# An encoder trunk on one core: a planner that reckons with later landing of copies between buffers and with shorter transposes, and two low parts of each layer's first quad on VectorE

## The chip, the cores and the metric

The kernel runs on 1 core of one Trainium2 chip. Five engines each run their own stream of instructions in order: TensorE (PE, with its weight loads listed as PEld), VectorE (DVE), ScalarE (ACT), GpSimd (POOL) and SyncE (SP); here POOL and SP mainly issue DMA transfers. The engines wait for each other by semaphores. The metric is the device time of one execution in microseconds; the median of several runs counts. Profiles come from one execution each.

## The reference

Two layers (DEPTH = 2) over one sequence of S = 512 tokens with D = 1024 channels, all in float32. In each layer:

```
h = rms_norm(x, attn_norm_g);  z = h @ w_in          # 1024 -> 512+128+128+512+512+512+1024+1024
qa, ka, va, qb, kb, vb, ga, gb = split(z)
qa, ka = rope(rms_norm(qa)), rope(rms_norm(ka));  qb, kb = rms_norm(qb), rms_norm(kb)
ya = window_gqa(qa, ka, va, sink) @ w_proj_a         # 8 heads of 64, 2 k/v heads, window 128
yb = neighbourhood_attn(qb, kb, vb, rel_bias) @ w_proj_b   # 8 heads, 8 x 64 grid, 8 x 16 window
x = x + (sigmoid(ga) * ya + sigmoid(gb) * yb) @ w_out
h = rms_norm(x, ffn_norm_g)
x = x + (silu(h @ w_gate) * (h @ w_up)) @ w_down     # hidden width 2816
```

## The kernel before, in words

**Precision and tiling.** Each float32 operand of a large product is split into a high part, rounded to a shorter format (fp32r), and a low part, the remainder. A product is then three matmuls on PE: high x high, high x low, low x high. x is kept transposed, 128 channels on the partitions and 512 tokens in a row. A projection goes by pairs of 128 output columns (`pair_matmul`) or by blocks of 128 tokens (`token_matmul`); weights come as slabs by DMA from POOL's queue, and their low parts by a second DMA that adds the weights onto the negated high part.

**Attention.** Head by head: scores on PE, maximum on DVE, exponential on ACT, scaling, transposes of the probabilities on PE, their split into high and low parts on ACT and DVE, products with v on PE. Two heads of 64 channels lie above each other on 128 partitions. `q_parts` puts q's high part on one half of the partitions and its low part on the other. `k_parts` (for the second branch four times a layer, for the first branch once) transposes k on PE, splits it on ACT and DVE, and then copies each of the four halves to the other half of the partitions by DMA on SP's queue:

```
Q.dma_start(kh[other].bitcast(F32), kh[own].bitcast(F32))
Q.dma_start(kl[other].bitcast(F32), kl[own].bitcast(F32))
```

Scores of the pair's first head read the first two of these copies. On SP's queue the small loads of the bias tables stand ahead of them.

**Feed-forward.** The first 256 hidden columns go as ordinary pairs (`evac_g`, `evac_u`), then five groups of 512 columns as "quads": seven products of quarter matrices in place of eight, in the order m = 1, 5, 6, 2, 7, 3, 4, for w_gate and for w_up. `Quad.high(m)` forms the sum of quarters that m needs (a11, a12, a21, a22 are the quarters of the raw weights) and rounds it on ACT; `high(6)` overwrites a21 and a11, `high(3)` overwrites a12. `Quad.low(m)` forms the low part. In most quads that is one subtraction on DVE; in the first quad's w_gate of each layer (`by_transfer`) it is `low_by_transfer`: ACT writes the negated high part, and a DMA from POOL's queue adds the source onto it, buffer to buffer. `chain_x` forms the seven sums and splits of x. On PE m = 1 and m = 5 come first; then `seed`, a COPY on ACT of the bank of m = 1, fills the bank into which m = 6 accumulates.

**What sets the order.** Nothing runs ahead of a recorded order. The function `trunk` is run twice. The first, dry run keeps a clock per engine, adds the `cost` of each operation, and notes in `ready` when each buffer is there; a DMA counts as landed some time after its bytes have moved. Beside the main stream of projection matmuls stand chains (generators: `chain_q`, `chain_kv`, `chain_pair_a`, `chain_pair_b`, `head`, `chain_x`, `chain_parts` and others). A chain yields a `Need`: the buffers, banks and events its next step wants. After each unit of three matmuls the planner issues those steps whose needs its clocks call met. So PE's order is an interleaving of projection matmuls with scores, transposes and products of the heads, chosen by the planner's costs. Weight loads, `high` and `low` hang on positions in the main stream (`at_pos`, `due`), not on clocks. The dry run also notes from when to when each buffer is used (`touch`); `Layout.pack` and `spread` then place all buffers in two arenas, in such a way that a buffer's place is not taken again at once. The second run emits the instructions in the order found.

All instructions are issued through one helper, so every row of the profile names its line, L308. Names tell rows apart: `arena` is either arena, `mm` are PSUM banks of projections, `at` PSUM banks of the attention and of transposes and m = 1 and 5, `cst` the constants with the identity.

Of the kernel before, what the change touches and what calls it, by code (L numbers as in the profile page):

```python
# [213 lines left out]
def trunk(ctx: ExitStack, tc: tile.TileContext, a: dict, out: bass.AP, lay: Layout):  # L214
# [20 lines left out]
    def buf(shape, dtype=F32):  # L235

        n = int(np.prod(shape))
        x = lay.place(n, dtype)
        t = arenas[dtype][:, x : x + n]
        if len(shape) == 2:  # L240
            t = t.rearrange("p (a b) -> p a b", b=shape[1])
        elif len(shape) == 3:
            t = t.rearrange("p (a b c) -> p a b c", b=shape[1], c=shape[2])
        return t

    def name_of(ap):
        return lay.owner(ap.offset) if ap.tensor.name in arena_names else ap.tensor.name
# [17 lines left out]
    ready = {}  # L265
    HOPS = {("pe", "dve"): 0.2, ("pe", "act"): 0.2, ("dve", "pe"): 0.26, ("act", "pe"): 0.3, ("dve", "dve"): 0.06}

    def at_(tensor, key):

        t, by = ready.get(tensor, (0.0, key))  # L270
        return t + HOPS.get((by, key), 0.0 if by == key else 0.15)


    def cost(eng, name, o, aps):
        n = max(x.free_size() for x in aps) / 1000.0
        in_psum = any(x.space == PS for x in aps[1:])
        if eng == "pe":
            cols = aps[2].free_size()
            if name == "transpose":
                return 0.11  # L280
            if aps[1].dtype == F32:
                return max(4 * cols, 256) / 2400.0 + 0.002
            return 0.12 if cols == 256 else (cols if cols >= 256 else 4 * cols) / 2255.0
        if eng == "act":
            return n * 0.833 + (0.06 if in_psum else 0.1) + 0.093 * sum(x.free_size() == 1 for x in aps[2:])
        if eng == "dve":
            fast = name in ("tensor_copy", "tensor_scalar") and not in_psum
            return n * (0.52 if fast else 6.4 if name == "reciprocal" else 1.04) + 0.075
        return n * 2.2 + 0.1
# [3 lines left out]
    def touch(aps, start, end):  # L293
        for x in aps:
            o = name_of(x)
            if isinstance(o, int):
                lay.touch(o, steps[0], start, end)

    class Engine:
# [3 lines left out]
        def __getattr__(self, name):  # L303
            f = getattr(self.eng, name)

            def call(*args, **kw):
                if not lay.dry:
                    f(*args, **kw)  # L308
                    return
                aps = [x for x in (*args, *kw.values()) if isinstance(x, bass.AP)]  # L310
                acc = kw.get("accum_out") if "accum_out" in kw else (args[7] if name == "tensor_tensor_reduce" else None)
                steps[0] += 1
                start = max([clock[self.key]] + [at_(name_of(x), self.key) for x in aps[1:]])
                if self.key == "dma":
                    start = max(start, clock["pe"] - 3.0)
                    if self.eng is nc.gpsimd:
                        clock["pool"] += 1.0
                    end = start + aps[0].free_size() * aps[0].shape[0] * 4 / 360e3
                    clock["dma"] = end
                    ready[name_of(aps[0])] = end + 2.0, "dma"  # L320
                    touch(aps, start, end + 2.0)
                    return
                end = start + cost(self.key, name, aps[0], aps)
                clock[self.key] = end
                ready[name_of(aps[0])] = end, self.key
                if acc is not None:
                    ready[name_of(acc)] = end, self.key
                touch(aps, start, end)

            return call  # L330
# [201 lines left out]
    def low_by_transfer(lo, src, h):  # L532

        A.activation(lo, h.bitcast(F32), AF.Copy, scale=-1.0)
        GQ.dma_start(lo, src, accum_op=ALU.add)

    class Quad:
# [37 lines left out]
        def low(self, m):  # L575
            src, h = self.parts[m]
            lo = buf([4, 256], F32R)
            if self.by_transfer:
                low_by_transfer(lo, src, h)
            else:  # L580
                V.tensor_tensor(lo, src, h.bitcast(F32), ALU.subtract)
            self.parts[m] = h, lo
# [503 lines left out]
    def layer(l):  # L1086
# [273 lines left out]
        def chain_x():  # L1360
# [26 lines left out]
            high(1, b11)  # L1387
            V.tensor_tensor(n1, b11, b12, ALU.subtract)
            yield from low(1)
            high(5, n1)  # L1390
            yield from normal(1)
            V.scalar_tensor_tensor(n2, n1, -1.0, b22, ALU.mult, ALU.subtract)
            high(6, n2)
            yield from low(5)
            yield from low(6)
            high(2, b21)
            yield from low(2)
# [194 lines left out]
```

## Time and profile before

| | |
|---|---|
| runs | 1484.63, 1482.7 and 1477.24 us, median 1482.7 |
| profiled execution | 1478.58 us, span 1476.8 us |
| mean granted PE clock | 0.983 |
| PE busy | 1405.2 us, 95% of the span |
| DVE, ACT, POOL busy | 62%, 48%, 25% |
| PE waits for ACT at `mm`, for copies between buffers at `at` | 24.9 us in 2 waits, 12.3 us in 7 waits |

In a row of a group or a timeline stand start and length in us (timeline), engine, operation, what it writes and reads with sizes, a count, and in brackets how long its engine was idle just before and what ended that. In a table of windows the last three columns are PE's granted clock (1.00 is full speed), the share of the DMA engines and GB/s. The span leaves out 1.8 us of the execution.

### The profile page before, as it was taken

The numbers are of one execution on the slowest core, as the hardware profiler recorded it, in microseconds if no ns is written. First come the engines' busy times: TensorE is split into PE (matmuls) and PEld (weight loads), VectorE is DVE, ScalarE is ACT, GpSimd is POOL, SyncE is SP. The second block draws the span as 40 slices with busy tenths as digits, with TensorE's granted clock in tenths as the row PEclk, the third lists the DMA queues.
The fourth block names the chain that finished last, engine by engine and source line by source line (L and its number), as shares of the span: only waits on it lengthen the run. The fifth ranks groups of instructions, "written<-read, shape, count | busy, mean of one in ns | idle before, by whom it ended". The sixth has DMA issues, their size and how long they took to land.

```text
span 1476.8 us, 21019 instructions
## 1 busy us (share of the span) xinstructions
PE 1405.2 (95%) x8074; PEld 1230.7 (83%) x8074; DVE 908.5 (62%) x1743; ACT 713.9 (48%) x1200; POOL 368.6 (25%) x374
## 2 busy tenths in 40 slices
PE   5999989999969999999999999999997999999998
PEld 4778878888869999999987887788886899999997
DVE  3876768543747565575647868673437575575653
ACT  3476657543544343433545775574345444343431
POOL 4533222234221110201353322123332211101111
PEclk9999999999989999999999999899999899999999
DMA  9877778899975745645798679669997754836455
GB/s 228 164 145 137 145 128 150 153 191 241 174 150 119 174 115 143 158 100 117 154 189 168 125 132 158 124 122 183 209 242 130 160 124 122 190 83 168 115 100 114
DMA packets 211427, 223.18 MB, mean 151 GB/s; under 512 B 25964, under 2 KB 179744, under 8 KB 211328
## 3 DMA queue, kind: packets, MB, share of 16 engines
q0 software_dynamic: 159920, 167.23, 61.1%
q1 hardware_dynamic: 51408, 54.62, 13.3%
q8 instruction: 63, 1.03, 0.3%
q14 instruction: 36, 0.29, 0.1%
HBM read 207.13 MB, written 2.10 MB: 142 GB/s over the span
## 4 chain that ended last, share of the span: by engine, by line
PE 69%; DMA 9%; DVE 9%; issue 7%; ACT 4%; POOL 2%; DVEq 0%; POOLq 0%; ACTq 0%; SPq 0%
PE mm L308 50%; PE at L308 19%; DVE arena L308 6%; ACT arena L308 4%; DMA arena<-arena 3%; DMA arena<-in_w_out 2%; DVE sm L308 2%; POOL arena L308 2%; DMA arena<-in_w_gate 1%; DMA arena<-in_w_up 1%; DMA arena<-in_rel_bias_b 1%; DMA vec<-in_q_norm_b 1%; DMA arena<-in_w_in 0%; ACT L308 0%; DVE hf L308 0%
## 5 line engine op out<-in xcount | busy, mean ns | idle before, releaser
L308 PE MATMUL mm<-arena 128*128 128x512 f32 (+1 forms) x5568 | 1127.9, 358 | 32.0 <-ACT mm L308 24.9
L308 PEld LDWEIGHTS mm<-arena 128*128 128x128 f32 x5568 | 910.1, 191 | 161.7 <-ACT mm L308 25.3
L308 PE MATMUL at<-arena 128*128 128x256 f32 (+2 forms) x1952 | 309.4, 299 | 15.1 <-DMA arena<-arena 12.3
L308 ACT ACTIVATE arena<-arena 128x1024 fp32r<-128x1024 f32 (+3 forms) x280 | 235.9, 865 | 176.9 <-DMA arena<-in_w_down 62.2
L308 ACT CAST arena<-arena 128x1024 fp32r<-128x1024 f32 (+2 forms) x250 | 211.7, 864 | 224.0 <-DVE arena L308 219.5
L308 PEld LDWEIGHTS at<-arena 128*128 128x128 f32 x1952 | 268.7, 193 | 38.7 <-DMA arena<-arena 11.9
L308 DVE TENSOR_TENSOR arena<-arena,arena 128x1024 fp32r<-128x1024 f32 (+2 forms) x236 | 228.3, 981 | 57.3 <-ACT arena L308 57.1
L308 POOL DMA_DIRECT2D arena<-in_w_in x168 | 168.4, 1367 | 368.3 <-ACT arena L308 367.9
L308 DVE TENSOR_TENSOR arena<-arena,mm 128x512 f32<-128x512 f32 x144 | 98.8, 686 | 255.9 <-PE mm L308 255.8
L308 POOL DMA_DIRECT2D arena<-in_w_down x96 | 98.2, 1210 | 503.2 <-ACT arena L308 388.4
L308 DVE TENSOR_TENSOR arena<-arena 128x1024 f32<-128x1024 f32 (+3 forms) x196 | 158.8, 824 | 19.2 <-DMA arena<-arena 14.1
L308 DVE TENSOR_TENSOR arena<-at,arena 128x384 fp32r<-128x384 f32 (+4 forms) x206 | 114.1, 562 | 52.7 <-ACT arena L308 45.9
L308 ACT CAST arena<-at 128x384 fp32r<-128x384 f32 (+2 forms) x164 | 74.4, 459 | 117.5 <-PE at L308 105.1
L308 PE MATMUL at<-cst,arena 128*128 128x128 f32 x504 | 87.4, 280 | 11.8 <-DVE arena L308 7.9
L308 PEld LDWEIGHTS at<-cst,arena 128*128 128x128 f32 x504 | 64.5, 143 | 30.5 <-DVE arena L308 10.9
L308 ACT ACTIVATE arena<-arena,negm 128x256 f32<-128x256 f32 (+1 forms) x128 | 71.6, 561 | 13.1 <-DVE negm L308 12.7
L308 DVE TENSOR_TENSOR arena<-mm,arena 128x512 f32<-128x512 f32 x72 | 49.3, 687 | 45.8 <-PE mm L308 45.7
L308 ACT COPY arena<-at 64x512 f32<-64x512 f32 (+1 forms) x60 | 34.8, 581 | 64.8 <-PE at L308 64.3
L308 POOL DMA_DIRECT2D arena<-in_w_out x32 | 35.2, 1292 | 54.5 <-ACT arena L308 54.5
L308 DVE CUSTOM_DVE_ANT_0 arena<-at,arena 128x256 f32<-128x256 f32 (+1 forms) x64 | 31.0, 486 | 28.7 <-PE at L308 28.4
L308 DVE CUSTOM_DVE_ANT_0 arena<-at,cst,nsnk 128x256 f32<-128x256 f32 (+1 forms) x64 | 34.3, 546 | 16.3 <-PE at L308 15.9
L308 DVE TENSOR_SCALAR arena<-arena,sm 128x384 f32<-128x384 f32 (+1 forms) x97 | 34.0, 405 | 1.1
(70 smaller groups left out, 444.2 us busy)
## 6 DMA issues: line engine op xcount, KB each, us to landing
arena<-in_w_in POOLq DMA_DIRECT2D x104, 512.0 KB, 7.1
arena<-in_w_down POOLq DMA_DIRECT2D x80, 512.0 KB, 6.8
arena<-in_w_gate SPq DMA_DIRECT2D x20, 1024.0 KB, 6.7
arena<-in_w_up SPq DMA_DIRECT2D x20, 1024.0 KB, 5.2
arena<-in_w_in POOLq DMA_DIRECT2D x64, 256.0 KB, 6.2
arena<-in_w_out POOLq DMA_DIRECT2D x32, 512.0 KB, 8.0
arena<-in_w_proj_a POOLq DMA_DIRECT2D x16, 512.0 KB, 8.8
arena<-in_w_proj_b POOLq DMA_DIRECT2D x16, 512.0 KB, 6.5
```

The source lines that it names most:

```text
L308: f(*args, **kw)
```

## The change

Three edits. In the planner's cost table a transpose counts 0.1 in place of 0.11 us. In its handling of a DMA, the result counts as there 7.0 us after its bytes have moved where the source is a buffer on the chip; from DRAM it stays 2.0. And in the quads with `by_transfer`, which is the first quad's w_gate in each layer, m = 1 and m = 2 get their low part by the subtraction on DVE, while 5, 6, 7, 3 and 4 stay with ACT and a DMA.

```diff
@@ -277,7 +277,7 @@
             if name == "transpose":
-                return 0.11
+                return 0.1
@@ -317,8 +317,9 @@
                     clock["dma"] = end
-                    ready[name_of(aps[0])] = end + 2.0, "dma"
-                    touch(aps, start, end + 2.0)
+                    end += 2.0 if aps[1].space == bass.MemoryType.DRAM else 7.0
+                    ready[name_of(aps[0])] = end, "dma"
+                    touch(aps, start, end)
                     return
@@ -575,7 +576,7 @@
             lo = buf([4, 256], F32R)
-            if self.by_transfer:
+            if self.by_transfer and m not in (1, 2):
                 low_by_transfer(lo, src, h)
             else:
                 V.tensor_tensor(lo, src, h.bitcast(F32), ALU.subtract)
```

The first two edits change no instruction, only the order and the places of buffers. In the attention this is PE's order before at the second branch's second pair in layer 0. `at ... <-cst` are transposes (the first row is k's tile), `mm` projection matmuls, `at` of 128x256 to 128x512 scores and products of heads, and the last row is the first score that reads this k:

```order
L308 MATMUL at_1857<-cst,arena_72 128x128 x4
L308 MATMUL mm_1837<-arena_73 128x512 x3
L308 MATMUL at_1869<-arena_73 128x512 x2
L308 MATMUL at_1872<-cst,arena_72 128x128 x2
L308 MATMUL mm_1837<-arena_73 128x512 x3
L308 MATMUL mm_1838<-arena_73 128x512 x6
L308 MATMUL at_1869<-arena_73 128x256 x2
L308 MATMUL at_1893<-cst,arena_72 128x128 x3
L308 MATMUL mm_1838<-arena_73 128x512 x6
L308 MATMUL at_1915<-arena_73 128x256 x2
```

And after, the same pair, from k's transposes on:

```order
L308 MATMUL at_1790<-cst,arena_72 128x128 x4
L308 MATMUL at_1795<-arena_73 128x512 x2
L308 MATMUL at_1798<-cst,arena_72 128x128 x2
L308 MATMUL mm_1662<-arena_73 128x512 x3
L308 MATMUL at_1809<-arena_73 128x384 x2
L308 MATMUL mm_1662<-arena_73 128x512 x3
L308 MATMUL at_1795<-arena_73 128x256 x2
```

then 14 rows of the same kinds, and these up to the first scores of that k:

```order
L308 MATMUL mm_1839<-arena_73 128x512 x6
L308 MATMUL mm_1838<-arena_73 128x512 x3
L308 MATMUL at_1889<-arena_73 128x256 x2
L308 MATMUL at_1912<-cst,arena_72 128x128 x3
L308 MATMUL at_1917<-arena_73 128x256 x2
```

Between the first and the last row there were 18 projection matmuls, and now there are 36; with them stand 16 products and scores (4 of 512 columns, 4 of 384, 8 of 256) in place of 4 (2 of 512, 2 of 256), and 15 transposes in place of 5. The k tile's transposes come earlier in the stream, the scores at much the same place. At the end of layer 0's attention the last head's last product stood 48 projection matmuls ahead of w_proj_a's first, and now 21.

At the first quad of layer 0, DVE before, from the evacuation of w_gate's ordinary pair on. The two rows of 128x1024 that write arena_73 are low parts of x, the first 128x4x256 is the add of `high(3)`, the rows with `mm` after it evacuate w_up's ordinary pair:

```order
L308 TENSOR_TENSOR arena_72<-mm_3281,arena_72 128x512
L308 TENSOR_TENSOR arena_72<-mm_3282,arena_72 128x512
L308 TENSOR_TENSOR arena_73<-arena_72,arena_73 128x1024 x2
L308 TENSOR_TENSOR arena_72<-arena_72 128x4x256
L308 TENSOR_TENSOR arena_72<-mm_3392,arena_72 128x512
L308 TENSOR_TENSOR arena_72<-arena_72 128x512
L308 TENSOR_TENSOR arena_73<-arena_72,arena_73 128x512
L308 TENSOR_TENSOR arena_73<-arena_72,arena_73 128x1024
L308 TENSOR_TENSOR arena_72<-arena_72 128x4x256
L308 TENSOR_TENSOR arena_72<-mm_3393,arena_72 128x512
```

And after:

```order
L308 TENSOR_TENSOR arena_72<-mm_3280,arena_72 128x512
L308 TENSOR_TENSOR arena_72<-mm_3281,arena_72 128x512
L308 TENSOR_TENSOR arena_73<-arena_72,arena_73 128x1024 x4
L308 TENSOR_TENSOR arena_72<-arena_72 128x4x256 x2
L308 TENSOR_TENSOR arena_72<-mm_3391,arena_72 128x512
L308 TENSOR_TENSOR arena_72<-arena_72 128x512
L308 TENSOR_TENSOR arena_73<-arena_72,arena_73 128x512
L308 TENSOR_TENSOR arena_72<-mm_3392,arena_72 128x512
```

`low(2)` stands at the head of a row of four low parts, and one low part of x and one subtraction of `chain_x` have moved ahead of w_up's evacuations. ACT at the same place before, up to the COPY that seeds the bank of m = 6; the first ACTIVATE row is the two Silu, the ACTIVATE rows of 128x1024 are negated high parts:

```order
L308 ACT_TABLE_LOAD
L308 ACTIVATE arena_72<-arena_72 128x512 x2
L308 ACTIVATE arena_73<-arena_73 128x1024
L308 CAST arena_73<-arena_72 128x1024 x2
L308 ACTIVATE arena_73<-arena_73 128x1024
L308 CAST arena_73<-arena_72 128x1024
L308 CAST arena_73<-arena_72 128x512
L308 ACTIVATE arena_73<-arena_73 128x1024
L308 CAST arena_73<-arena_72 128x1024
L308 CAST arena_73<-arena_72 128x512
L308 CAST arena_73<-arena_72 128x1024 x2
L308 COPY mm_3500<-at_3466 128x512
```

And after:

```order
L308 ACT_TABLE_LOAD
L308 ACTIVATE arena_72<-arena_72 128x512 x2
L308 CAST arena_73<-arena_72 128x1024 x2
L308 ACTIVATE arena_73<-arena_73 128x1024
L308 CAST arena_73<-arena_72 128x1024 x2
L308 CAST arena_73<-arena_72 128x512
L308 ACTIVATE arena_73<-arena_73 128x1024
L308 CAST arena_73<-arena_72 128x512
L308 CAST arena_73<-arena_72 128x1024
L308 COPY mm_3496<-at_3464 128x512
```

Two instructions fewer stand ahead of the COPY: the activation of `low(2)` and one cast of 128x1024, which now follows the COPY. On POOL's queue the copies from buffer to buffer around the quad go from seven to five. Layer 1 has the same order at this place.

## The prediction

> **What bounds the kernel now.** I read the page first, then the table of waits, then single stretches of the timeline with the granted clock beside them. The page's head, its busy times and the shares of the chain that ended last:
>
> ```profile
> span 1476.8 us, 21019 instructions
> PE 1405.2 (95%) x8074; PEld 1230.7 (83%) x8074; DVE 908.5 (62%) x1743; ACT 713.9 (48%) x1200; POOL 368.6 (25%) x374
> PE 69%; DMA 9%; DVE 9%; issue 7%; ACT 4%; POOL 2%; DVEq 0%; POOLq 0%; ACTq 0%; SPq 0%
> ```
>
> PE is busy for 1405.2 of 1476.8 us. The change takes no matmul away and adds none, so it can only win from the 71.6 us in which PE stands, and from stretches in which PE runs at a lower clock after it stood. The waits of PE that the change can touch (us in total, times, longest):
>
> ```profile
> PE mm L308 <- ACT mm L308: 24.9, 2, 12.5
> PE at L308 <- DVE arena L308: 12.5, 20, 2.1
> PE at L308 <- DMA arena<-arena: 12.3, 7, 4.2
> ```
>
> Two places carry 37.2 us of PE's idle time: two waits of 12.5 us, one in each layer's first quad, and seven waits for copies between buffers, all in the attention. The first stands like this in layer 0 (timeline; start, length, engine):
>
> ```profile
> 403.04 1.28 DVE L308 TENSOR_TENSOR arena<-mm,arena 128x512 f32<-128x512 f32 x2
> 404.23 1.28 ACT L308 ACT_TABLE_LOAD   x1
> 404.23 2.35 DVE L308 TENSOR_TENSOR arena<-arena,arena 128x1024 fp32r<-128x1024 f32 x2
> 405.52 2.10 ACT L308 ACTIVATE arena<-arena 128x512 f32<-128x512 f32 x3
> 406.06 5.91 PE L308 MATMUL at<-arena 128*128 128x256 f32 x48
> 407.53 1.98 ACT L308 CAST arena<-arena 128x1024 fp32r<-128x1024 f32 x2
> 408.00 1.28 POOL L308 DMA_DIRECT2D arena<-arena  x1 [10.78 <-ACT arena L308]
> 409.41 1.05 ACT L308 ACTIVATE arena<-arena 128x1024 fp32r<-128x1024 f32 x1
> 413.53 1.22 DVE L308 TENSOR_TENSOR arena<-arena 128x1024 f32<-128x1024 f32 x1 [6.94 <-DMA arena<-arena]
> 414.67 0.68 DVE L308 TENSOR_TENSOR arena<-mm,arena 128x512 f32<-128x512 f32 x1
> 415.46 0.69 DVE L308 TENSOR_TENSOR arena<-arena 128x512 f32<-128x512 f32 x1
> 416.19 0.62 ACT L308 CAST arena<-arena 128x512 fp32r<-128x512 f32 x1 [0.31 <-DVE arena L308]
> 423.74 0.57 ACT L308 COPY mm<-at 128x512 f32<-128x512 f32 x1
> 424.36 5.49 PE L308 MATMUL mm<-arena 128*128 128x256 f32 x24 [12.39 <-ACT mm L308]
> ```
>
> DVE stops for 6.94 us until 413.53. What stands there is the add of `high(3)`, which overwrites a12; the copy issued at 408.00 still reads a12 for `low(2)`. Behind the add on DVE wait the two evacuations of w_up's first pair, behind them casts on ACT, and behind those the COPY that seeds the bank of m=6. PE finishes m=1 and m=5 at 411.97 (406.06 + 5.91) and stands until 424.36.
>
> The second place, at a k pair of layer 0 and at two of layer 1 (timeline), and what the chain of waits shows ahead of the first and the last of them:
>
> ```profile
> 195.88 0.60 PE L308 MATMUL at<-cst,arena 128*128 128x128 f32 x4
> 202.66 0.35 PE L308 MATMUL at<-arena 128*128 128x256 f32 x1 [0.77 <-DMA arena<-arena]
> 207.18 0.58 PE L308 MATMUL at<-arena 128*128 128x256 f32 x1 [4.17 <-DMA arena<-arena]
> ```
> ```profile
> 917.69 0.35 PE L308 MATMUL at<-arena 128*128 128x256 f32 x1 [1.42 <-DMA arena<-arena]
> 919.73 0.58 PE L308 MATMUL at<-arena 128*128 128x256 f32 x1 [1.68 <-DMA arena<-arena]
> 950.14 0.58 PE L308 MATMUL at<-arena 128*128 128x256 f32 x1 [3.20 <-DMA arena<-arena]
> ```
> ```profile
> 199.30 7.84 DMA arena<-arena
> ...
> 943.54 7.43 DMA arena<-arena
> ```
>
> k is transposed at 195.88, and the last copied half has landed at 207.14 (199.30 + 7.84): 11.3 us, of which 7.84 is the copy. The next scores need it and PE stands. These three pairs hold nearly all of the 12.3 us. After such a stop PE's granted clock (last but two in a row) is halved for a while:
>
> ```profile
> 207.00:209.00 2.00, 1.82 (x5) 1.53 (x6) 0.43 (x2) 0.00 (x0) 0.00 (x0) 0.50 0.38 57
> 211.00:212.00 1.00, 1.00 (x4) 0.81 (x3) 0.45 (x2) 1.00 (x3) 0.00 (x0) 0.53 0.32 51
> 424.00:430.00 6.00, 5.64 (x26) 5.64 (x27) 2.15 (x3) 3.33 (x5) 3.20 (x3) 0.50 0.52 119
> 921.00:925.00 4.00, 4.00 (x14) 3.64 (x13) 1.89 (x6) 1.81 (x6) 0.00 (x0) 0.50 1.10 219
> 925.00:927.00 2.00, 2.00 (x12) 1.76 (x11) 0.43 (x2) 0.72 (x3) 0.00 (x0) 0.92 0.02 4
> 953.00:956.00 3.00, 3.00 (x11) 2.52 (x11) 0.79 (x3) 1.38 (x4) 0.00 (x0) 0.50 1.11 238
> ```
>
> **The attention.** The new landing of 7.0 us and the transposes' 0.1 us change no instruction of it, only the order. Counted in the order shown with the change, PE had 18 matmuls of 512 columns, 2 score matmuls of 512 and 2 of 256, and 5 transposes between this k's transposes and its first scores; now it has 36, 2+2 of 512, 4 of 384, 8 of 256 and 15 transposes. Their durations:
>
> ```profile
> 284.68 18.54 PE L308 MATMUL mm<-arena 128*128 128x512 f32 x81
> 444.28 2.92 PE L308 MATMUL at<-arena 128*128 128x256 f32 x23
> ```
>
> That is 0.229 us for 512 columns and 0.127 for 256; 384 lie between, at 0.18, and a transpose of 128 columns is put at 0.09 (below 0.127). Before: 20 x 0.229 + 2 x 0.127 + 5 x 0.09 = 5.3 us. Now: 40 x 0.229 + 4 x 0.18 + 8 x 0.127 + 15 x 0.09 = 12.2 us. Needed were 11.3 at this pair, the longest copy that I found on the chain. The other late pairs go from 5.3 to 6.5 and 7.8 us up to 10.6 and 12.9 by the same count. So six of seven waits go. The half clock behind them goes too: 4.7 us at this pair (207.18 to about 211.9), 5.6 at the second (919.73 to about 925.3), and about as much at the third (950.14 to 956 at the least). Half of 15.9 us is lost, 8.0. Term: 12.3 + 8.0 = 20.3, less about 1.3 for the pair with 10.6 us of cover, 19.0. Bounds: 0 if the copies land later by as much as they are given, 20.3 if all goes; below nothing it goes only by new waits, a rival below.
>
> What is late next is the end of the attention: the last head's products now end 21 matmuls of 0.229 us (4.8 us) ahead of the first product of w_proj_a, where it were 48 in layer 0. The last head's parts are read only 24 matmuls later, by w_proj_b, so 45 x 0.229 = 10.3 us cover the last copy, add, cast and subtraction (four steps of 0.6 to 0.7 us, by the 512-column rows above, with 0.2 between). That stays hidden, at 0. On SP's queue the copies stay behind the same bias loads as before. The dry run also places all buffers of both arenas anew; a buffer that then comes free too late would be a new wait, and as nothing here shows one, I put it at 0 (the lost cover would be one of the rivals' stops, below).
>
> The skill has a rule on this clock. The Trainium skill, TensorE: Matmul & The Clock Gate, section "What's actually happening", says that an idle window of about 3.4 us halves the clock and about 3.4 us of work bring it back. The 4.7 to 5.6 us of these rows are longer; by that page each of the three stops would give back 1.7 us in place of 2.7, and the sum would be 27.6 and the time 1455.1.
>
> **The first quad.** Per layer it removes two ACT activations of 1.05 us, two POOL issues of 1.28 and two copies of 512 KB from buffer to buffer, and adds two DVE subtractions of 1.2. The removed ones lie beside PE's matmuls, on engines that are busy 48% and 25%: 0. `low(1)` falls where DVE waits for PE anyway:
>
> ```profile
> 382.60 0.69 DVE L308 TENSOR_TENSOR arena<-arena,mm 128x512 f32<-128x512 f32 x1 [2.03 <-PE mm L308]
> ```
>
> 2.03 us cover 1.2, so 0; without that cover 1.2 on a DVE that has idle time before 403. `low(2)` lands on the path, in front of x's lows. With the rows above, on DVE: evacuations end 404.3; three lows of 1.18 end 407.8; the fourth waits for the two casts of ACT, which lost the activation ahead of them (405.52, two Silu of the three rows' 2.10 less 1.05, and 1.98: 408.6) and ends 409.8; two adds of 1.17 end 412.1, the first of which waits for no copy any more; evacuation and product 0.68 + 0.69, 413.5; cast 0.62, 414.2; subtraction 0.7, 414.9; the second evacuation and product, 416.3; cast 417.0; a CAST of 1.04, 418.0; COPY 0.57, 418.6. PE goes on at 418.6 in place of 424.36: 5.8 us per layer, 11.6 in all (the wait of layer 1 is 12.5). 6.6 us of waiting stay, and I let the half clock after it stay as it is. Bounds per layer: -2.4 (both subtractions on the path, and the add held by something else) to 12.4 plus half of the 6 us at half clock, 15.4. I take 5.8, since each of its steps has a row.
>
> **Sum.** 19.0 + 11.6 = 30.6 us. The profiled execution's own time is 1478.6, 1.8 above its span, and stands 4.1 under the median of 1482.7. Against the execution it gives 1448; against the median, 1452.1. I forecast 1452.
>
> **Rivals.**
> - Only the quad gains. For it: the median copy of 128 KB is quick (last number), and where one is late something else may delay it.
>
> ```profile
> arena<-arena POOLq DMA_DIRECT2D x14, 512.0 KB, 6.9
> arena<-arena SPq DMA_DIRECT2D x40, 128.0 KB, 3.2
> ```
>
> Then cover of 5.3 us would have done, the late copies are late by what shares the rings and queues with them, and the new order runs into that again. 1482.7 - 11.6 = 1471. [...] Against: the chain ends in copies of 7.43 and 7.84 at the late pairs, and it is these that count. 0.15.
> - Only the attention gains: the add finds another thing to wait for (the cast of a11 or the raw weights), and 12.4 stays. 1482.7 - 19 = 1464. Against: DVE's wait in the row names the copy. 0.09.
> - The change does nothing: each wait passes to the next thing. 1482. 0.05.
> - Slower: the new order puts more heads' steps at once on DVE, and PE waits there for scores and products in the middle of the attention. PE already waits 20 times for DVE, by 0.6 us on average. A longer stop costs what these did, (12.3 + 8.0) / 3 = 6.8 us with its clock; five of them eat 34, and from six on (41) it is slower by over half a per cent: 1452 + 41 = 1493. Against: the number of DVE and ACT instructions in the attention is the same, and DVE is busy 62%. 0.10.
> - Better: in the quad nearly all goes, the clock too, 9 us more per layer: 1434. 0.04.
>
> **How the numbers follow.** The forecast itself has 0.57, with its own range from 1446 to 1460: 20 or 16 in the attention, 2 us either way per quad, and the 4 us between execution and median. For 8 in 10 the range goes from 1444 to 1474 and takes in the two half gains, 0.57 + 0.15 + 0.09. Half a per cent, 7.4 us, is about what a measurement of this kernel can tell from no change. Faster: 0.57 + 0.15 + 0.09 + 0.04 = 0.85; same 0.05; slower 0.10.
>
> **What would show it.** Right: among PE's waits the copies are down from 12.3 to under 2 us, and the clock after k's first scores is whole; DVE has no wait for a copy at the first quad; PE's wait for the seeding COPY is 6 to 7 us in both layers, still with half clock behind. Wrong: PE's waits for DVE or ACT in the attention grow by more than 10 us, or the copies take as much longer as they are issued earlier; or in the quad another engine's row stands ahead of the COPY. If PE's busy time grows although the matmuls are the same, the clock fell somewhere new.

## The result, and the profile after

The changed kernel takes 1444.7 us (median of four runs, 1439.9 to 1445.1) against 1482.1 before (four runs, one more than above, 1477.2 to 1484.6): a ratio of 0.974, 95% interval 0.9716 to 0.9764, or 37.4 us less by the medians. 1452 was forecast, 31 us less; the medians lie at the low end of the range, and 0.974 times 1482.1 is 1443.6, just under it. Two executions of kernels tested below, of 1969 and 3562 us, took far longer than all others of their kernels and are in no median. The two profiled executions are 1478.6 and 1444.7 us long, their spans 33.9 us apart. The page's head of the kernel after, its busy times and the shares of its chain:

```profile
span 1442.9 us, 20988 instructions
PE 1394.6 (97%) x8074; PEld 1224.6 (85%) x8074; DVE 912.2 (63%) x1752; ACT 706.8 (49%) x1191; POOL 363.4 (25%) x370
PE 77%; DVE 12%; issue 3%; DMA 3%; ACT 3%; POOL 1%; DVEq 0%; POOLq 0%; ACTq 0%
```

PE stands for 48.3 us (1442.9 less 1394.6) where it stood for 71.6, and it is busy 10.6 us less with the same matmuls, most of it because fewer of them ran at half clock (8.3 us, below). Its waits (us in total, times, longest):

```profile
PE mm L308 <- ACT mm L308: 12.5, 2, 6.3
PE at L308 <- DVE arena L308: 11.5, 15, 2.3
```

The row of PE waiting for copies between buffers, 12.3 us before, is gone, and the two waits for the seeding COPY are half as long. At the attention's pair that stood for 4.17 us before, PE now works through at full clock (table of windows, granted clock last but two):

```profile
203.00:207.00 4.00, 4.00 (x22) 3.54 (x21) 3.05 (x12) 3.54 (x10) 2.03 (x2) 1.00 0.59 122
207.00:209.00 2.00, 2.00 (x13) 1.67 (x12) 1.97 (x8) 1.47 (x4) 0.00 (x0) 1.00 1.03 145
```

The first quad of layer 0 (timeline):

```profile
396.30 1.28 DVE L308 TENSOR_TENSOR arena<-mm,arena 128x512 f32<-128x512 f32 x2
...
397.50 3.48 DVE L308 TENSOR_TENSOR arena<-arena,arena 128x1024 fp32r<-128x1024 f32 x3
...
399.53 5.91 PE L308 MATMUL at<-arena 128*128 128x256 f32 x48
399.84 1.98 ACT L308 CAST arena<-arena 128x1024 fp32r<-128x1024 f32 x2
...
401.85 1.22 DVE L308 TENSOR_TENSOR arena<-arena,arena 128x1024 fp32r<-128x1024 f32 x1 [0.87 <-ACT arena L308]
402.99 2.35 DVE L308 TENSOR_TENSOR arena<-arena 128x1024 f32<-128x1024 f32 x2
...
405.26 0.68 DVE L308 TENSOR_TENSOR arena<-mm,arena 128x512 f32<-128x512 f32 x1
...
410.99 0.57 ACT L308 COPY mm<-at 128x512 f32<-128x512 f32 x1
...
411.61 5.49 PE L308 MATMUL mm<-arena 128*128 128x256 f32 x24 [6.17 <-ACT mm L308]
```

DVE goes from the evacuations through four low parts and two adds to w_up's evacuation without a wait for a copy. Between the two profiles the waits fell by 24.7 us (12.3 for copies, 12.4 for the COPY). The time that PE's work lost to half clock, added up over windows of 2 us as busy time times one less the granted clock, fell from 14.0 to 5.7 us, by 8.3. That is 33.0 of the 33.9 us. Behind the two waits for the COPY the half clock stayed (6.0 us of PE's work lost there before, 5.7 now). One stop is longer than before: ahead of the second norm's sums of squares in layer 0, PE stands 2.34 us at 380.33, where it stood 0.26.

### The profile page after: what moved, and what is told of

The parts are those of the page before. It is cut to its first block, busy times and chain, and to the rows that moved or that the text cites. A ratio compares the mean times of both kernels' runs of the same rounds, so it can differ in the third digit from the quotient of the medians.

```text
span 1442.9 us, 20988 instructions
## 1 busy us (share of the span) xinstructions
PE 1394.6 (97%) x8074; PEld 1224.6 (85%) x8074; DVE 912.2 (63%) x1752; ACT 706.8 (49%) x1191; POOL 363.4 (25%) x370
## 4 chain that ended last, share of the span: by engine, by line
PE 77%; DVE 12%; issue 3%; DMA 3%; ACT 3%; POOL 1%; DVEq 0%; POOLq 0%; ACTq 0%
PE mm L308 60%; PE at L308 18%; DVE arena L308 9%; ACT arena L308 3%; DVE sm L308 3%; DMA arena<-in_w_in 2%; DMA arena<-in_w_up 1%; POOL arena L308 1%; DMA cst<-in_consts 1%; DVE hf L308 0%; DVE den L308 0%; ACT L308 0%; ACT mm L308 0%; ACT sm L308 0%; DVEq L308 0%
## 5 line engine op out<-in xcount | busy, mean ns | idle before, releaser
L308 PE MATMUL mm<-arena 128*128 128x512 f32 (+1 forms) x5568 | 1123.6, 357 | 20.7 <-ACT mm L308 12.5
L308 ACT ACTIVATE arena<-arena 128x1024 fp32r<-128x1024 f32 (+3 forms) x276 | 232.7, 862 | 188.8 <-DMA arena<-in_w_down 58.9
L308 PE MATMUL at<-arena 128*128 128x256 f32 (+2 forms) x1952 | 303.8, 296 | 5.0 <-DVE arena L308 3.5
L308 PEld LDWEIGHTS at<-arena 128*128 128x128 f32 x1952 | 265.7, 191 | 25.9 <-DVE arena L308 8.1
L308 DVE TENSOR_TENSOR arena<-arena,arena 128x1024 fp32r<-128x1024 f32 (+2 forms) x240 | 233.0, 984 | 59.7 <-ACT arena L308 59.3
L308 DVE TENSOR_SCALAR arena<-arena,sm 128x384 f32<-128x384 f32 (+1 forms) x102 | 33.9, 387 | 1.1
```

## The experiments

**Each edit alone.** The three edits are put into the kernel before one by one.

```diff
-            if self.by_transfer:
+            if self.by_transfer and m not in (1, 2):
```

> Kernel before with the quad edit alone: low(1) and low(2) of the first w_gate quad on DVE, the planner's numbers as before. My theory (two separate gains that add up): PE's two waits for the seeding COPY fall from 12.4 to 6.2 us each and nothing else moves, since the edit saves no clock there; the attention keeps its waits for copies. That is 12.4 us, a ratio of about 0.992. Rival (the quad gains only where the order of the attention was repaired too, or the run after gains by the new places of the buffers): the waits for the COPY stay above 10 us and the time is within 0.3% of before.

1467.0 us against 1482.3 in the same session, a ratio of 0.9902 (0.9871 to 0.9933). The gain, 15.3 us by the medians, is what was expected or somewhat more. A second profile of this kernel:

> The kernel with the quad edit alone, profiled a second time, since the granted clock of its first profile was 0.658 throughout. The edit gained 14.5 us by the timed runs where I gave it 12.4. My theory: the waits for the COPY are about 6.2 us each and the waits for k copies 11 to 15 us as in the kernel before. Rival: the waits for k copies have fallen too, by the new places of the buffers.

This execution was a long one, 1474.4 us. Waits of PE:

```profile
PE at L308 <- DMA arena<-arena: 15.3, 6, 4.7
PE mm L308 <- ACT mm L308: 10.1, 2, 5.0
```

The waits for the COPY fell, those for k copies did not. So the quad edit gains by itself.

```diff
-                    ready[name_of(aps[0])] = end + 2.0, "dma"
-                    touch(aps, start, end + 2.0)
+                    end += 2.0 if aps[1].space == bass.MemoryType.DRAM else 7.0
+                    ready[name_of(aps[0])] = end, "dma"
+                    touch(aps, start, end)
```

> Kernel before with the landing of 7.0 us for copies between buffers alone; transposes at 0.11, all low parts of the first quad by transfer. My theory: the seven waits of PE for copies go (12.3 us) and the half clock after them (8.3 us of PE's busy time), while the two waits of 12.4 us at the first quads stay: 20.6 us, a ratio of about 0.986. Rival (the two numbers of the planner are only right together): with the old transpose cost another order comes out, with copies that are still late or with waits for DVE, and less than 12 us are gained.

1461.7 us, 0.9867 (0.9838 to 0.9896): 20.6 us less, as expected. In its profile PE waits for no copy between buffers, and 24.4 us for the COPY. That the size is met so exactly is partly luck: between the profiles it is 17.8 us, of which 12.3 are the waits, while the half clock fell by 5.5 us (14.0 to 8.5) and not by 8.3, since some followed stops at the two norms of layer 0 in this execution.

```diff
-                return 0.11
+                return 0.1
```

> Kernel before with the transpose at 0.1 us in the planner alone. My theory: it only shifts the order a little, the k copies are planned as late as before, and all waits stay in size: within 0.4% of before, either way. Rival (this number carries the gain in the attention): the waits for copies fall by more than half and the ratio is 0.993 or less.

1473.1 us, 0.9941 (0.9923 to 0.996). My theory falls: this number gains 9 us by itself. The rival is not right either, since in the profile the waits for copies are still 10.9 us. The profiled execution took 1479.6 us, 6.5 above the median of the runs, so the kernel was profiled a second time:

> The kernel with the transpose edit alone, profiled a second time, since its first profile (1479.6 us) stood 6.5 us above the median of its runs. My theory (the first profile caught late copies of the first quads' low parts: the waits for the COPY were 15.9 us each): now they are about 12.4 us each, and the span is about 7 us shorter. Rival (the difference lies in the attention or in the clock): the COPY waits are again near 15.9 us, and the rest differs.

1469.6 us. Its waits:

```profile
PE mm L308 <- ACT mm L308: 30.2, 2, 15.2
DVE arena L308 <- DMA arena<-arena: 19.5, 4, 6.9
PE at L308 <- DMA arena<-arena: 8.6, 6, 2.8
```

The waits for the COPY are as long as in the first profile, so the difference between the two executions does not lie there, against what I expected. Against the kernel before, the copies cost 3.7 us less, PE's waits for DVE 4.8 less (7.7 for 12.5) and the half clock 6.5 less (7.5 for 14.0), and the COPY costs 5.3 more; together that is 9.7 us, and the two executions lie 9.0 apart. PE's two waits for the COPY grew by 2.8 and 2.5 us; ahead of each layer's first quad DVE now waits for one more copy between buffers (timeline), and the chain that ends in the COPY stands behind that:

```profile
395.94 2.74 DVE L308 SCALAR_TENSOR_TENSOR arena<-arena,vecT 128x512 f32<-128x512 f32 x4 [2.88 <-DMA arena<-arena]
...
1114.64 2.74 DVE L308 SCALAR_TENSOR_TENSOR arena<-arena,vecT 128x512 f32<-128x512 f32 x4 [2.78 <-DMA arena<-arena]
```

Of the waits for DVE, a stop at the start is gone. PE there sums the squares of x for the first norm (matmuls that read `ones`), first in this kernel, then in the kernel before:

```profile
42.84 1.02 PE L308 MATMUL at<-ones,arena 128*128 128x1 f32 x8
```
```profile
45.38 1.02 PE L308 MATMUL at<-ones,arena 128*128 128x1 f32 x8 [2.06 <-DVE arena L308]
```

**The kernel before, once more.**

> The kernel before, unchanged, profiled a second time. My theory (what differs between its runs is when copies between buffers land): the same PE waits at the same places, those for k copies and the two for the COPY, with sizes that differ by some us in all from the first profile's 12.3 and 24.9. Rival (the runs differ in the granted clock or at the start): these sums agree within 1 us, and the difference lies in PE's busy time or ahead of the first matmuls.

This execution is 8.2 us longer than the first profiled one (span 1485.0). The copies cost 14.5 in place of 12.3 us, the COPY 23.4 in place of 24.9, and the stop ahead of the second norm's sums in layer 0 1.91 in place of 0.26: together 2.4 us. The larger part is PE's busy time, 1410.5 in place of 1405.2. Windows behind the stop of 2.06 us at the first norm, in this execution and, at about the same place with the same stop, in the first one:

```profile
46.00:48.00 2.00, 2.00 (x10) 1.90 (x10) 1.15 (x7) 1.08 (x2) 0.61 (x1) 0.50 0.00 0
48.00:50.00 2.00, 2.00 (x6) 1.61 (x5) 1.26 (x8) 0.00 (x0) 2.00 (x4) 0.50 0.24 32
50.00:52.00 2.00, 2.00 (x6) 1.52 (x5) 1.80 (x11) 0.98 (x2) 1.35 (x2) 0.50 1.08 156
52.00:54.00 2.00, 2.00 (x10) 1.63 (x10) 0.38 (x2) 1.18 (x3) 0.00 (x0) 0.81 1.28 280
```
```profile
46.00:48.00 2.00, 2.00 (x12) 1.72 (x12) 1.21 (x8) 0.75 (x2) 1.03 (x2) 1.00 0.02 4
48.00:50.00 2.00, 2.00 (x10) 1.35 (x9) 1.69 (x12) 1.72 (x4) 2.00 (x4) 1.00 0.48 53
```

The same stop of 2.06 us brought 6.8 us at half clock in one execution (three windows of 2 us at 0.50, one at 0.81: 3.4 us lost) and none in the other. So the rival holds for the larger part, though the sums do not agree within 1 us as it asked: these two executions differ by where the half clock falls, and less by when copies land.

**Two edits together.** First the changed kernel without the landing, then without the transpose's new cost.

```diff
-                    end += 2.0 if aps[1].space == bass.MemoryType.DRAM else 7.0
+                    end += 2.0
```

> Changed kernel with the landing of copies between buffers back at 2.0 us; the transpose at 0.1 and the quad edit stay. My theory (the landing alone repairs the attention; the transpose edit gains by the start of each layer): the waits for k copies stay at 10 to 13 us, the waits for the COPY are about 12 us in two, and the ratio is 0.980 to 0.986. Rival (with the quad edit the transpose edit gains as much as both numbers): below 0.978.

1453.3 us, 0.9816 (0.9784 to 0.9849), in the range of my theory. PE waits 9.9 us in 7 times for k copies and 12.5 us for the COPY. The landing then adds 8.6 us to reach the changed kernel, where alone it gained 20.6. Against the kernel before of its own session this kernel gains 27.8 us; the quad edit alone gained 15.3, so the transposes' number brings 12.5 us here, more than alone. That fits the row above: DVE's wait of 2.9 us for a copy ahead of the quad is absent here.

```diff
-                return 0.1
+                return 0.11
```

> Changed kernel with the transpose back at 0.11 us in the planner; landing 7.0 and the quad edit stay. It completes the eight combinations of the three edits but one. Alone the transpose edit gained 9 us, and the landing gained 9 us on top of the other two but 20 alone. Theory A (both repair the same waits for k copies, so with the landing in place the transposes have little left): within 0.3% of the changed kernel. Theory B (the transposes' gain is another one, the stop of PE ahead of each norm's sums and the half clock after it, which the landing does not touch): 4 to 9 us more than the changed kernel, with stops of 1 to 2 us at the matmuls that read the ones.

1446.7 us, 0.9775 (0.975 to 0.98), against 0.974 (0.9716 to 0.9764) with it: 2 us by the medians, 5 by the ratios, 3.2 by the gains of 34.2 and 37.4 us over the kernel before of each one's own session, and the intervals overlap. How large the transpose's share is in the whole is not settled. Its stop is there again in the profile of this kernel (timeline, and the windows from 45 to 51 us):

```profile
46.27 1.73 PE L308 MATMUL at<-ones,arena 128*128 128x1 f32 x8 [2.06 <-DVE arena L308]
```
```profile
45.00:51.00 6.00, 4.73 (x16) 4.09 (x17) 4.65 (x23) 1.45 (x3) 3.15 (x4) 0.62 0.30 56
```

The stop is the one that Theory B names, and this execution, 1450.8 us, was the longest of the four. But the changed kernel has a stop of its own at the second norm's sums, 2.34 us at 380.33, where this one has 0.15, so part of the gain is given back there. In all PE stands 48.4 us here and 48.3 in the changed kernel; the two spans differ by PE's busy time.

**How much landing it takes, and low(1).**

```diff
-                    end += 2.0 if aps[1].space == bass.MemoryType.DRAM else 7.0
+                    end += 2.0 if aps[1].space == bass.MemoryType.DRAM else 4.5
```

> Changed kernel with a landing of 4.5 us in place of 7.0. My theory (each late k pair needs about 11 us between its transposes and its scores, and the landing buys that time nearly one to one): the cover falls to about 9 us and waits for copies of 2 to 6 us come back, 3 to 9 us more than the changed kernel with the half clock. Rival (any landing above the median copy of 3.2 to 4.0 us is enough): no wait for copies above 1 us in all, and the time of the changed kernel within 0.2%.

1445.3 us, 0.9777 (0.9744 to 0.9809), by the median the time of the changed kernel. PE's wait for copies:

```profile
PE at L308 <- DMA arena<-arena: 0.8, 3, 0.4
```

The rival is right. By the order and the prediction's durations, the cover at the three pairs that were late is 8.1, 7.8 and 9.3 us here, less than the 11.3 that I took to be needed, and it suffices but for 0.8 us.

```diff
-            if self.by_transfer and m not in (1, 2):
+            if self.by_transfer and m != 2:
```

> Changed kernel, but low(1) of the first w_gate quad goes by ACT and a copy again; low(2) stays on DVE. My prediction's view (low(1) lies beside PE's matmuls either way): the time is that of the changed kernel within 0.2%. Rival (the copy of low(1), which reads a11, holds the add of high(6) on DVE and with it all that DVE does ahead of the first quad; the profile with the transpose edit alone shows such a wait of 1.68 us, the kernel before one of 0.19): 2 to 5 us more than the changed kernel, with a wait of DVE for a copy between buffers ahead of the quad.

1442.6 us, 0.9757 (0.9723 to 0.9792): no difference from the changed kernel that these runs show. As far as they show, `low(1)` costs nothing either way, as predicted, and the gain of the quad edit is that of `low(2)`.

**What is left of the first quad's wait.** From here on the changed kernel is the base. First the split of w_up's ordinary pair goes later, and `chain_x` waits for the COPY to be issued:

```diff
-            h, lo = act(F32R), act(F32R)
-            split(gt[j], h, lo)
-            u.append((h, lo))
+            soon(lambda: u_parts(j), 6.0)
...
             yield from low(2)
+            yield Need(keys=[f"{key}seed"], backlog=XLOG)
```

> Changed kernel, and at the first quad the splits of w_up's ordinary pair (two casts and two subtractions of 512 columns) come 6.0 us later in the main stream, and chain_x goes on behind x's low part 2 only once the seeding COPY is issued. So on ACT two casts that wait for DVE and one of 1024 columns no longer stand ahead of the COPY. My theory (the COPY waits in ACT's queue behind work that nobody needs yet): PE's wait there falls from 6.2 to about 2.4 us, and as that is short, the half clock behind it (3 us lost per layer) goes or shrinks: 7 to 14 us less than the changed kernel, 1431 to 1438 us. Rival (the wait only moves): PE then stands as long at m=7 for x's low part 7, or at m=2, and the time is that of the changed kernel within 0.3%.

1445.7 us, 0.9771 (0.9736 to 0.9807): the wait moved. In layer 0 (timeline):

```profile
404.69 4.58 PE L308 MATMUL mm<-arena 128*128 128x256 f32 x24 [2.64 <-ACT mm L308]
...
414.75 13.13 PE L308 MATMUL mm<-arena 128*128 128x256 f32 x84 [2.57 <-DVE mm L308]
```

The wait for the COPY fell from 6.2 to 2.6 us as my theory had it, but m=7 then waits 2.6 us for the second seed, which DVE forms behind a subtraction (`seed_c`: the sum of m=6's bank and a copy of m=5's goes into the bank of m=3, and m=7 goes on in m=6's bank, so it must wait until that has been read). Half clock followed each, and nothing was won. In the next kernel three more things are put later, and `low(4)` goes on DVE:

```diff
-                early = max(0.0, early - 1.2)
+                early = max(0.0, early - 2.7)
...
-            if self.by_transfer and m not in (1, 2):
+            if self.by_transfer and m not in (1, 2, 4):
...
-            soon(lambda: u_parts(j), 6.0)
+            soon(lambda: u_parts(j), 11.0)
...
             yield from low(7)
+            yield Need(keys=[f"{key}seed_c"], backlog=XLOG)
```

> The kernel with the COPY ahead of the late splits, and three edits more: the splits come 11.0 us later in place of 6.0, chain_x's parts 3 and 4 wait until the second seed (of m=3's bank) is issued, and the first w_gate quad prepares its later parts later (the lead shrinks by 2.7 us from part to part, not by 1.2; low(4) then goes on DVE). So fewer casts stand ahead of the COPY on ACT, and fewer subtractions ahead of the second seed on DVE. My theory (the order on ACT and DVE, not their amount of work, holds PE there): both waits, 2.6 us each in both layers, fall under 1 us, the half clock behind them goes, and the time is 1430 to 1437 us. Rival (DVE has more to do there than PE's matmuls cover, so the waits go on to m=2, m=7 or m=3): within 0.3% of the changed kernel or slower.

1435.55 us, 0.9706 (0.9682 to 0.9731): 9.2 us under the changed kernel by the medians, and its four runs lie between 1435.4 and 1435.7. PE's waits at the two first quads are now:

```profile
PE mm L308 <- DVE mm L308: 6.1, 2, 3.0
...
PE mm L308 <- DMA arena<-arena: 1.9, 2, 1.1
```

The wait for the COPY is gone from the list. The second seed still costs 3.0 us a layer, against what I expected, but the half clock is down to 2.8 us of PE's work in the whole kernel. So order, not amount, held PE at the COPY. No other kernel that computes the reference was faster; the next two are level with this one. Then all that stood ahead of the second seed was moved behind it:

```diff
-                quads[l, q, w].due(m, total[0] - early)
+                quads[l, q, w].due(m, total[0] - early + (5.4 if early and m == 3 else 0.0))
...
-            soon(lambda: u_parts(j), 11.0)
+            soon(lambda: u_parts(j), 11.5 if j else 16.5)
...
-            yield Need(keys=[f"{key}seed"], backlog=XLOG)
+            yield Need(keys=[f"{key}fetch"], backlog=XLOG)
```

> The kernel with the later preparation, and of the second seed (DVE reads m=6's bank and a copy of m=5's bank that ACT makes) all that is not needed yet is taken away from in front: that copy comes ahead of the casts of 1024 columns on ACT, the splits of w_up's pair come 11.5 and 16.5 us later, high(3) and low(3) of the first quad 5.4 us later, low(3) on DVE. My theory (only order holds PE there): PE's wait for the second seed falls from 3.0 to below 1 us per layer, a wait of about 1 us may come at m=3, and the time is 1428 to 1434 us. Rival (DVE's work there is more than PE's matmuls cover): the wait appears at m=3 or m=4 in full, and the time stays within 0.2% of 1435.6.

1434.8 us, 0.9693 (0.967 to 0.9716). In this kernel the two blocks of w_up's ordinary pair enter w_down in swapped order: it does the same work, but each block meets the weights of the other, so it does not compute the reference, and only its order and time count here. The second seed no longer holds PE, but the waits passed on. In layer 0 (timeline):

```profile
407.92 3.45 PE L308 MATMUL mm<-arena 128*128 128x256 f32 x25
412.43 3.25 PE L308 MATMUL mm<-arena 128*128 128x256 f32 x24 [1.06 <-DVE arena L308]
415.89 1.30 PE L308 MATMUL mm<-arena 128*128 128x512 f32 x3 [0.22 <-DVE arena L308]
418.76 5.12 PE L308 MATMUL mm<-arena 128*128 128x512 f32 x32 [1.57 <-DVE arena L308]
```

The first row is m=7 and one matmul of m=3, which then waits 1.06 us for a low part; the rows of 512 columns are w_down's first products, which wait 1.57 us for the late splits. With the blocks in their own order:

> The kernel with the last splits, with the two blocks of w_up's ordinary pair entering w_down in their own order (in the run of that kernel they were swapped, with the same work). Expected: the same time as there, 1434.8 us within 0.2%, and against the kernel with the later preparation (1435.6) no difference, since the wait for the second seed passed on to waits of 1.1 and 1.6 us for DVE at m=7 and m=3. Rival: the swapped order hid a wait at the first group of w_down, and 1 to 3 us are added.

1436.8 us (1434.6 to 1439.8), 0.971 (0.9682 to 0.9737): the same within these runs, and no gain over the kernel with the later preparation. The rival's wait is there, 1.25 us for the cast of the block that is split last. Whether another order would bring these last 3 to 4 us a layer too, or DVE and ACT have more to do there than PE's matmuls cover, was not settled.

## Why the prediction was right and where it was wrong

**The bound and the mechanisms were right.** PE sets the time, and nearly all of the difference between the two profiles (32.7 of 33.9 us) came from the two places named. The copies went from PE's waits, the clock there is whole, and DVE no longer waits for a copy at the quad.

**The first quad.** 5.8 us per layer were forecast, 6.2 came (12.39 to 6.17 in layer 0, 12.50 to 6.29 in layer 1). The working holds step by step. In it DVE's evacuations end at 404.3, the two adds at 412.1 and the COPY at 418.6; 6.7 us earlier, where layer 0's quad now lies, that is 397.6, 405.4 and 411.9, and the rows have 397.6, 405.3 and 411.6. The half clock behind the wait stayed, as said. `low(1)` at nothing was right.

**The attention.** 19.0 us were forecast; the profiles show 12.3 of waits and all of the 8.0 of clock, 20.3. The 1.3 that I kept back for the pair with 10.6 us of cover was too careful. The 11.3 us "needed" were one execution's time from transposes to landing at one pair; the kernel with a landing of 4.5 shows that covers of 7.8 to 9.3 us nearly do.

**The step that failed: the transposes' cost, priced at nothing of its own.** I took both numbers of the planner for one effect in the attention and gave them one term. The runs show that the transposes' number does something else as well. The stop of 2.06 us ahead of the first norm's sums stands in five profiles of kernels with 0.11 (the kernel before twice, the quad edit alone in its second profile, the landing alone, the changed kernel without the transposes) and in none of the ten with 0.1. It costs its 2.06 us and the half clock behind it, which took from nothing to 3.4 us of PE's work in those five. It was in my own list, as the longest of 20 waits for DVE (12.5 us in all), which I did not take apart. By medians, each against the kernel before of its own session, the transposes' number gains 9.2 us alone and 3.2 on top of the other two edits: alone it also shortens waits for k copies, which the landing repairs too. Without it the gain is 34.2 us, and the interval of that ratio (0.975 to 0.98, or 30 to 37 us) takes in my 30.6; with it the gain is 37.4, and the interval (35 to 42 us) does not. The exact share stays open, since the intervals overlap.

**And the base of the sum.** Between the profiles my 30.6 stand against 33.9: 1.3 us from the attention, 0.8 from the quads, the rest from elsewhere. Little of the transposes' gain shows there, because the first norm's stop brought no half clock in the first profile and a stop at the second norm came in its place. I then put the sum against the median, 4.1 us above the profiled execution, as if those 4.1 us stayed. The second profile of the kernel before shows what a longer execution of it holds: more half clock (18.8 us of PE's work lost against 14.0), behind the first norm's stop and behind a longer one at the second. Some of that the change takes away too. That this makes up the 3.5 us between 33.9 and 37.4 is argued from one long execution, not shown run by run.

**The clock rule.** From the Trainium skill, TensorE: Matmul & The Clock Gate, section "What's actually happening", the three stops in the attention would by my estimate have given back 1.7 us each; the profile's were 2.4 to 2.8. Two stops of the second profile gave 1.7 and 1.6 (at 930 and 960 us). On the idle window of about 3.4 us that the prediction took from that section, the runs differ: in the kernel with the COPY ahead of the late splits a clock of 0.50 followed stops of 2.64 and 2.57 us. The page also says that the window is free-running and does not reset when a kernel starts. The first norm's stop of 2.06 us, with 6.8 us of half clock once and none another time, agrees with that.

**The rivals.** The slower one did not come: PE's waits for DVE went from 12.5 to 11.5 us. "Only the quad gains" falls with the landing alone (20.6 us), "only the attention gains" with the quad edit alone (15.3). The better one did not come either, since a wait of 6.2 us and the half clock behind it stayed in each layer.

## What to carry to other kernels

Where a planner lays out the order, a wrong landing time costs its wait and the half clock behind it; here 4.5 us, a little above the median copy of 3.2 us in the profile before, did as well as 7.0, and 2.0 did not. A low part or a copy that still reads a buffer is paid by whoever overwrites the buffer next and by all that stands behind that on its engine, so look at what is queued there before moving work to a queue that is idle. Take apart a row of many small waits before pricing an edit at nothing, and take one profiled execution as one draw: what makes other executions longer may be the very stops that a change removes.

## What the runs showed of the hardware

A stop of PE of 2 us can cost 2 us or 5.4: in two executions of one kernel the same stop of 2.06 us was followed by no half clock and by 6.8 us of it. Four runs of the kernel before spread over 7.4 us (1477.2 to 1484.6), the changed kernel's four over 5.2, those of the kernel with the later preparation over 0.3, and those of the last kernel over 5.2 again. It is therefore not shown that fewer stops bring the runs closer together.

Half clock between the second norm and the first quad is partly paid back at the COPY. In the kernel with only `low(2)` on DVE, these are PE's two waits for the COPY, in layer 0 and layer 1 (timeline), and behind them a window after each of the two norms (granted clock last but two):

```profile
408.93 5.49 PE L308 MATMUL mm<-arena 128*128 128x256 f32 x24 [6.46 <-ACT mm L308]
...
1114.10 4.64 PE L308 MATMUL mm<-arena 128*128 128x256 f32 x24 [4.98 <-ACT mm L308]
```
```profile
380.00:382.00 2.00, 2.00 (x11) 1.56 (x10) 1.72 (x10) 0.14 (x1) 0.86 (x1) 1.00 1.04 152
...
1084.00:1086.00 2.00, 2.00 (x6) 1.52 (x6) 1.66 (x11) 1.62 (x2) 0.05 (x1) 0.50 1.05 150
```

In other kernels with `low(2)` on DVE it is the same: where half clock fell there, the wait was 5.0 us (both layers of the landing of 4.5 and of the quad edit alone), where none did 6.2 to 6.3 (both layers of the changed kernel and of the changed kernel without the landing, and without the transposes). A stop at that norm with no half clock after it, 2.34 us in the changed kernel, left the wait at 6.17. In the kernel before, the COPY's wait in layer 0 was 12.39 us in one profile and 10.96, behind such half clock, in the other.
